# Full-row second products in the attention scores of a hybrid decoder trunk

## The chip, the cores and the metric

The kernel runs on one core of one Trainium2 chip. The metric is the device time of one execution in microseconds (us). A core has a matrix engine (PE, with its weight loads shown as PEld), a vector engine (DVE), a scalar engine (ACT), GpSimd (POOL) and a queue for transfers (SP). Each of them takes its instructions in the program's order, and they wait for each other through semaphores.

## The reference, cut to what matters

The trunk has two layers for 512 tokens of width 1024: a pooling layer with a convolutional gated feed-forward, then differential attention with a second feed-forward. The part at issue is the attention's scores. Each of 8 heads has two queries and two keys (c = 0, 1) of 64 channels:

```python
def block(args):
    qi, i = args
    s = jnp.einsum('bqchd,bkchd->bchqk', qi, k).astype(jnp.float32) * sm_scale
    qpos = i * Q_BLOCK + jnp.arange(Q_BLOCK)
    mask = kpos[None, :] <= qpos[:, None]
    s = jnp.where(mask, s, jnp.finfo(jnp.float32).min)
    p = jax.nn.softmax(s, axis=-1)
    attn = p[:, 0] - lam_full * p[:, 1]
    return jnp.einsum('bhqk,bkhe->bqhe', attn.astype(v.dtype), v)
```

A block is 128 queries, so there are 4 blocks a head and 32 units (h, qi) in all; block qi looks at the first (qi + 1) x 128 keys.

## The kernel before

All large products split each operand into a high and a low part, whose sum is the operand, and take three products of the parts (`mm3`, lines 158 to 160: high x high, high x low, low x high). PE's order is written out by hand; the order of DVE, ACT, POOL and SP in the attention is made by a scheduler when the program is built.

`heads(p)` makes the queries and keys of two heads, p in 0 to 3. Both projections come out with the channels of head 2p on partitions 0 to 63 (`lower`) and those of head 2p + 1 on 64 to 127 (`upper`). For the query, one tile `qs` of 128 rows holds the high part on the head's own half and the low part on the other half. For the key there are two kinds of tile: `kh`, one for each head, that holds the high part on both halves, and `kl`, one for both heads, that holds the low part of each head on its own half. So the scores of one unit and one c are two products into one bank, in `scores`:

```python
nc.tensor.matmul(ps[:, :m], qs[h, c][:, q], k1[:, :m], start=True, stop=False)
nc.tensor.matmul(ps[:, :m], qs[h, c][hi, q], k2[hi, :m], start=False, stop=True)
```

The first (line 526) contracts 128 rows: (query high + query low) x key high. The second (line 527) contracts the head's own 64 rows: query high x key low. `m` is 256, 256, 384 and 512 columns for qi = 0 to 3. A unit thus has four products on PE, one after the other: high and low for c = 0, high and low for c = 1.

The softmax of a unit runs on DVE (line 531, scale, mask and maximum, one for each c), ACT (line 533, the exponential) and DVE again (lines 538 to 540, the difference of the two softmaxes into `e`). The loop over the units takes at step i the scores of unit i, then some steps of a `filler` (projections of later heads `pj_q` and `pj_k`, values `pv`, the output product `pw`), then the transposes `pa` of unit i - 2 (line 549), the products `po` of unit i - 3 with the values (line 556) and, for the last block of a head, two steps later the transposes `pt` of that head's normed output `on` (line 574).

Before each projection POOL multiplies the 128x1024 chunk of weights by the norm's gain (line 479, `raw_q` and `raw_k`). It also takes the reciprocal root in each head's norm (lines 180 and 181, `r_o`), for which DVE's `on` (line 568) waits. Nothing else runs on POOL while the scores are taken.

Tiles of 128x512 such as `qs`, `kh` and `kl` come from one pool with the tag T and 44 slots. At the end of the first feed-forward its activations fill all 44. A slot is free for a new tile when the last reader of the tile before it has run.

Of the kernel before, what the change touches and what calls it, by code (L numbers as in the profile page):

```python
# [8 lines left out]
F32 = mybir.dt.float32  # L9
# [32 lines left out]
def constants():  # L42
    """What depends on shapes alone: the identity; the causal mask, whose last 128 columns are a
    diagonal block (rows are queries, columns keys); and for each pooling window the matrices, rows
    tokens in and columns tokens out, that take the mean over the window less the token: within the
    first tile of tokens, within a later one, and from the tile before it."""
    import numpy as np

    a = np.arange(P)
    back = a[None, :] - a[:, None]  # L50
    mask = np.zeros((P, S), np.float32)
    mask[:, S - P:] = np.where(back > 0, np.float32(NEG), np.float32(0))
    first, later, before = [], [], []
    for w in WINDOWS:
        near = (back >= 0) & (back < w)
        count = np.minimum(a + 1, w)[None, :]
        first.append(np.where(near, 1 / count, 0) - np.eye(P))
        later.append(np.where(near, 1 / w, 0) - np.eye(P))
        before.append(np.where(back[:, :16] + P < w, 1 / w, 0))
    return np.concatenate([np.eye(P), mask, *first, *later, *before], axis=1).astype(np.float32)  # L60
# [3 lines left out]
def trunk(ctx, tc, x, norm_g, pool_w, pool_scale, kv_norm, w_kv, wq, lam, subln_g, wo,  # L64
          w_up, conv_w, conv_b, w_down, final_norm, consts, out):
    nc = tc.nc
# [11 lines left out]
    def big(name, dt=F32R):  # L78
        return tp.tile([P, S], dt, tag="T", bufs=44, name=name)
# [13 lines left out]
    def spread(v, n):  # L93
        """[128, a] as [128, a, n]"""
        return v.unsqueeze(2).to_broadcast([P, v.shape[1], n])

# [1 line left out]
    xt = [const.tile([P, D], F32, name=f"x{t}") for t in range(NT)]  # L98
# [14 lines left out]
    def across(src, name):  # L113
        """A vector over the channels, on every partition, in halves."""
        halves = [big(f"{name}{i}", F32) for i in range(2)]
        for i in range(2):
            nc.sync.dma_start(out=halves[i], in_=src[i * S:(i + 1) * S].unsqueeze(0).to_broadcast([P, S]))
        return halves

    # TensorE's clock rises with its use  # L120
    ones = const.tile([P, P], F32, name="ones")
# [16 lines left out]
    def split(src, hi, lo):  # L138
        """hi + lo is src exactly, each in the 12 bits that one pass of TensorE carries."""
        nc.scalar.copy(hi, src)  # L140
        nc.vector.tensor_tensor(lo, src, hi, ALU.subtract)  # L141

    def split_scaled(src, by, hi, lo):
        """The same of src times a scalar for each partition."""
        nc.scalar.activation(hi, src, AF.Copy, scale=by)
        nc.vector.scalar_tensor_tensor(lo, src, by, hi, ALU.mult, ALU.subtract)

    def chunk(src, a, b, name):
        """[128, a, b] of weights, and where their parts go."""
        raw = wp.tile([P, a * b], F32, tag="raw", bufs=3, name=f"raw_{name}")  # L150
        hi = wp.tile([P, a * b], F32R, tag="hi", bufs=5, name=f"hi_{name}")
        lo = wp.tile([P, a * b], F32R, tag="lo", bufs=5, name=f"lo_{name}")
        nc.sync.dma_start(out=v3(raw, a), in_=src)
        return raw, hi, lo
# [10 lines left out]
    def columns(loaded):  # L165
        """Per-channel vectors, loaded as rows, with a channel a partition."""
        r, n, name = loaded
        ps = bank(f"pv_{name}")
        nc.tensor.transpose(ps[:, :n], r[:n, :], ident[:n, :n])
        c = const.tile([P, n], F32, name=f"c_{name}")  # L170
        nc.vector.tensor_copy(c, ps[:, :n])
        return c

    def rstd_of(ssq, n, name, eps=None):
        """From the mean of the squares."""
        r = small([P, n], f"r_{name}")
        if eps is None:
            nc.gpsimd.tensor_scalar(r, ssq, EPS, None, ALU.add)
        else:
            nc.gpsimd.tensor_tensor(r, ssq, eps, ALU.add)  # L180
        nc.gpsimd.tensor_tensor(r, r, halfneg[:, :n], ALU.pow)
        return r

    def rms(t, name):
        """One over the root mean square of x[t], and room for x[t]."""
        sq = wide(f"sq_{name}{t}")
        ssq = small([P, 1], f"ssq_{name}{t}")
        nc.scalar.activation(sq, xt[t], AF.Square, scale=D ** -0.5, accum_out=ssq)
        return rstd_of(ssq, 1, f"{name}{t}"), [sq[:, :S], sq[:, S:]]

    def normed(t, r, h, g=None):
        """x[t] over its root mean square, tokens on partitions, in halves of the channels."""
        for i in range(2):
            c = slice(i * S, (i + 1) * S)
            if g is None:
                nc.vector.tensor_scalar(h[i], xt[t][:, c], r, None, ALU.mult)
            else:
                nc.vector.scalar_tensor_tensor(h[i], xt[t][:, c], r, g[i], ALU.mult, ALU.mult)

    class Normed:  # L200
        """Normed x, channels on partitions, split; a tile of tokens at a time, in the steps rms,
        scale, turn and split."""

# [48 lines left out]

# [1 line left out]
    pscale = across(pool_scale[0], "pscale")  # L254
# [92 lines left out]

    # The steps, by tile of tokens, group of channels or chunk of weights, in the order in which
    # each engine takes its part of them.
    steps = dict(a=pool_rms, h=pool_scaled, g=gains, m=pool_weights, x=pool_weights_split, i=pool_in,  # L350
# [6 lines left out]

# [1 line left out]
    def ffn(l, hT, cw, ws, pss, after):  # L359
        """`pss` hold the first products, with `ws`, for half of the tokens. after(t, half) is called  # L360
        when that half of x[t] is done."""
        act = []
# [69 lines left out]

# [1 line left out]
    gkv, gsub = shared  # L434
# [12 lines left out]
    lamf = const.tile([P, 1], F32, name="lamf")  # L447
    # minus lambda
    nc.vector.tensor_tensor(lamf, lexp[:, 1:2], lexp[:, 0:1], ALU.subtract)
# [41 lines left out]
    def heads(p):  # L491
        """Queries and keys of two heads. A query's parts lie on the two halves of the partitions,
        and the keys' high parts on both, so that one product takes both parts of the query."""
        for c in range(2):
# [8 lines left out]
            ps = yield from project(w_kv[:, col:col + P], gkv, f"k{p}{c}")  # L503
            k2 = big(f"kl{p}{c}")
            for i, hi, lo in ((0, lower, upper), (1, upper, lower)):
                k1 = big(f"kh{p}{c}{i}")
                nc.scalar.copy(k1[hi], ps[hi])
                nc.scalar.copy(k1[lo], ps[hi])
                nc.vector.tensor_tensor(k2[hi], ps[hi], k1[hi], ALU.subtract)
                ks[2 * p + i, c] = (k1, k2, hi)  # L510
            yield
# [3 lines left out]
    def scores(h, qi):  # L515
# [7 lines left out]
        for c in range(2):  # L523
            ps = bank(f"sc{h}{qi}{c}")
            k1, k2, hi = ks[h, c]
            nc.tensor.matmul(ps[:, :m], qs[h, c][:, q], k1[:, :m], start=True, stop=False)  # L526
            nc.tensor.matmul(ps[:, :m], qs[h, c][hi, q], k2[hi, :m], start=False, stop=True)  # L527
            # minus the scaled scores, and minus their maximum
            e = e01[:, c * S:(c + 1) * S]
# [5 lines left out]
            e2.append(e[:, :n])  # L535
        # In units of the first softmax's sum, of which sub_norm takes account.
        r = small([P, 1], f"rs{h}{qi}")
# [85 lines left out]

    # The steps of the blocks of queries are taken apart, and other products put between them, so
    # that TensorE need not wait for the softmax.
    filler = chain(lambda: heads(1), lambda: heads(2), lambda: value_steps(1), lambda: heads(3),
# [6 lines left out]
    def behind(i):  # L633
        """The later steps of earlier blocks, at step i."""
        u = i - VALUES
# [14 lines left out]
    def wo_last():  # L650
        """What does not need the last head for the first two tiles of tokens."""
        wo_weights(6)
        wo_weights(7)
        for t in range(2):
            for dh in range(2):
                begun[t, dh] = bank(f"pw6{t}{dh}")
                wo_part(begun[t, dh], t, dh, 6, True, False)
                yield 0.25
# [99 lines left out]
```

## Time and profile before

| | us |
|---|---|
| median of 3 runs | 1044.49 |
| lowest and highest run | 1044.32 and 1048.61 |
| span of the profiled execution | 1043.1 |
| PE busy in the span | 1031.1 (99%) |
| DVE busy | 571.1 (55%) |
| ACT busy | 428.1 (41%) |
| POOL busy | 78.3 (8%) |

The profiled execution is one execution on the chip. Its span reaches from its first to its last instruction, so the span is compared with spans and the median with medians. A PE row of the timeline begins where the product begins, or where its weight load begins if PE had to wait for that load; its end is modelled, and rows overlap. What a product takes of PE's time is read from the distance between the starts of neighbouring rows, not from the row's own length.

### The profile page before, as it was taken

How to read it: one execution, taken by the hardware profiler on the slowest of the kernel's cores; microseconds unless marked ns; L12 is line 12 of the kernel's file. 1: busy time of each engine (PE TensorE's matmuls, PEld its weight loads, DVE VectorE, ACT ScalarE, POOL GpSimd, SP SyncE). 2: the span in 40 equal slices, each digit the busy share in tenths (PEclk: the TensorE clock that was granted, in tenths of full speed). 3: DMA queues.
4: the chain of work that ended last, by engine and by line, in shares of the span. 5: the costliest groups of instructions: out<-in, count | busy, mean ns of one | idle time of the engine just before them, and what ended most of it. 6: DMA issues, size and time to landing. Idle time of an engine off the chain costs nothing.

```text
span 1043.1 us, 12315 instructions
## 1 busy us (share of the span) xinstructions
PE 1031.1 (99%) x4871; PEld 843.4 (81%) x4871; DVE 571.1 (55%) x873; ACT 428.1 (41%) x671; POOL 78.3 (8%) x97
## 2 busy tenths in 40 slices
PE   8999999999999999999999999999999999999997
PEld 8988888888888887877777777898888888888885
DVE  5776566565621325366756676866656656532313
ACT  5454434443421124356545653444443444322211
POOL 4500000000000003330210000100000000000001
PEclk8999999999999999999999999999999999999999
DMA  8333333333323322241203102243333233323312
GB/s 250 106 109 93 101 101 88 95 101 101 93 94 101 93 99 81 65 138 61 62 21 101 61 21 61 67 116 90 93 101 100 88 95 101 101 82 100 101 41 80
DMA packets 128707, 95.33 MB, mean 91 GB/s; under 512 B 3329, under 2 KB 111498, under 8 KB 128650
## 3 DMA queue, kind: packets, MB, share of 16 engines
q1 hardware_dynamic: 128650, 94.55, 29.8%
q8 instruction: 38, 0.62, 0.2%
q14 instruction: 19, 0.16, 0.1%
HBM read 92.44 MB, written 2.10 MB: 91 GB/s over the span
## 4 chain that ended last, share of the span: by engine, by line
PE 97%; DVE 1%; DMA 1%; POOL 0%; ACT 0%; SPq 0%; issue 0%; DVEq 0%; POOLq 0%; ACTq 0%
PE pu L158 16%; PE pu L159 15%; PE pu L160 15%; PE pd L158 8%; PE pd L159 8%; PE pd L160 8%; PE sc L527 2%; PE po L556 2%; PE pj_k L158 2%; PE sc L526 2%; PE pw L158 2%; PE pj_q L158 2%; PE pw L160 1%; PE pj_k L160 1%; PE pj_q L159 1%; PE pj_q L160 1%
## 5 line engine op out<-in xcount | busy, mean ns | idle before, releaser
L141 DVE TENSOR_TENSOR lo_u<-raw_u,hi_u 128x1024 fp32r<-128x1024 f32 x84 | 103.0, 1229 | 130.5 <-ACT hi_u L140 130.5
L158 PE MATMUL pu<-n1h,hi_u 128*128 128x512 f32 (+1 forms) x384 | 144.1, 375 | 0.0
L159 PE MATMUL pu<-n3l,hi_u 128*128 128x512 f32 (+1 forms) x384 | 144.0, 375 | 0.0
L158 PE MATMUL pu<-n3h,hi_u 128*128 128x512 f32 (+1 forms) x384 | 143.6, 374 | 0.0
L160 PE MATMUL pu<-n1h,lo_u 128*128 128x512 f32 (+1 forms) x384 | 143.3, 373 | 0.0
L160 PE MATMUL pu<-n3h,lo_u 128*128 128x512 f32 (+1 forms) x384 | 142.1, 370 | 0.0
L159 PE MATMUL pu<-n1l,hi_u 128*128 128x512 f32 (+1 forms) x384 | 142.0, 370 | 0.0
L158 PE MATMUL pd<-hi_d,ah 128*128 128x512 f32 x352 | 138.8, 394 | 0.0
L159 PE MATMUL pd<-lo_d,ah 128*128 128x512 f32 x352 | 138.7, 394 | 0.0
L160 PE MATMUL pd<-hi_d,al 128*128 128x512 f32 x352 | 138.7, 394 | 0.0
L141 DVE TENSOR_TENSOR lo_d<-raw_d,hi_d 128x1024 fp32r<-128x1024 f32 x44 | 53.9, 1226 | 152.7 <-ACT hi_d L140 152.7
L140 ACT CAST hi_u<-raw_u 128x1024 fp32r<-128x1024 f32 x84 | 88.0, 1050 | 68.0 <-PE pu L159 62.9
L140 ACT CAST hi_d<-raw_d 128x1024 fp32r<-128x1024 f32 x44 | 46.1, 1048 | 148.0 <-PE pd L160 136.5
L158 PEld LDWEIGHTS pu<-n3h,hi_u 128*128 128x128 f32 x384 | 72.1, 188 | 14.1
L160 PEld LDWEIGHTS pu<-n1h,lo_u 128*128 128x128 f32 x384 | 72.0, 188 | 14.1
L160 PEld LDWEIGHTS pu<-n3h,lo_u 128*128 128x128 f32 x384 | 72.1, 188 | 13.4
L159 PEld LDWEIGHTS pu<-n1l,hi_u 128*128 128x128 f32 x384 | 72.1, 188 | 13.4
L158 PEld LDWEIGHTS pu<-n1h,hi_u 128*128 128x128 f32 x384 | 72.2, 188 | 12.0
L159 PEld LDWEIGHTS pu<-n3l,hi_u 128*128 128x128 f32 x384 | 72.2, 188 | 11.9
L160 PEld LDWEIGHTS pd<-hi_d,al 128*128 128x128 f32 x352 | 65.8, 187 | 16.3
L158 PEld LDWEIGHTS pd<-hi_d,ah 128*128 128x128 f32 x352 | 65.8, 187 | 16.3
L159 PEld LDWEIGHTS pd<-lo_d,ah 128*128 128x128 f32 x352 | 65.8, 187 | 16.2
(148 smaller groups left out, 1570.6 us busy)
## 6 DMA issues: line engine op xcount, KB each, us to landing
raw_u<-in_w_up_dram SPq DMA_DIRECT2D x88, 512.0 KB, 3.9
raw_d<-in_w_down_dram SPq DMA_DIRECT2D x44, 512.0 KB, 3.4
raw_v<-in_w_kv_dram SPq DMA_DIRECT2D x8, 512.0 KB, 3.5
raw_q<-in_wq_dram SPq DMA_DIRECT2D x8, 512.0 KB, 4.0
raw_k<-in_w_kv_dram SPq DMA_DIRECT2D x8, 512.0 KB
raw_o<-in_wo_dram SPq DMA_DIRECT2D x8, 512.0 KB, 4.1
x<-in_x_dram SPq DMA_DIRECT2D x4, 512.0 KB
out_dram<-y SPq DMA_DIRECT2D x8, 256.0 KB, 2.1
```

What stands on the lines that cost most here:

```text
L140: nc.scalar.copy(hi, src)
L141: nc.vector.tensor_tensor(lo, src, hi, ALU.subtract)
L158: nc.tensor.matmul(ps, lh, rh, start=first, stop=False)
L159: nc.tensor.matmul(ps, lh, rl, start=False, stop=False)
L160: nc.tensor.matmul(ps, ll, rh, start=False, stop=last)
L526: nc.tensor.matmul(ps[:, :m], qs[h, c][:, q], k1[:, :m], start=True, stop=False)
L527: nc.tensor.matmul(ps[:, :m], qs[h, c][hi, q], k2[hi, :m], start=False, stop=True)
L556: nc.tensor.matmul(po[h][:, qi * P:(qi + 1) * P], aT[:, kt * P:(kt + 1) * P], vt[kt][h // 4][:, (h % 4) * VD:(h % 4 + 1) * VD], start=kt = ...
```

## The change

The key's low part gets a tile for each head. The half that belongs to the head holds the low part, and the other half is set to zero by POOL (a new line 507, which makes 16 instructions of 64x512). The second product of the scores then takes all 128 rows: the other rows of the query meet zeros. The number of products, their columns and their order are as they were. The comments and docstrings are blanked out too, which adds one line ahead of `heads`' loop, so line 509 of before is line 510 of after, and lines 526 and 527 become one line 527.

```diff
             ps = yield from project(w_kv[:, col:col + P], gkv, f"k{p}{c}")
-            k2 = big(f"kl{p}{c}")
             for i, hi, lo in ((0, lower, upper), (1, upper, lower)):
-                k1 = big(f"kh{p}{c}{i}")
+                k1, k2 = big(f"kh{p}{c}{i}"), big(f"kl{p}{c}{i}")
+                nc.gpsimd.memset(k2[lo].bitcast(F32), 0.0)
                 nc.scalar.copy(k1[hi], ps[hi])
                 nc.scalar.copy(k1[lo], ps[hi])
                 nc.vector.tensor_tensor(k2[hi], ps[hi], k1[hi], ALU.subtract)
-                ks[2 * p + i, c] = (k1, k2, hi)
+                ks[2 * p + i, c] = (k1, k2)
...
-            k1, k2, hi = ks[h, c]
-            nc.tensor.matmul(ps[:, :m], qs[h, c][:, q], k1[:, :m], start=True, stop=False)
-            nc.tensor.matmul(ps[:, :m], qs[h, c][hi, q], k2[hi, :m], start=False, stop=True)
+            for last, k in enumerate(ks[h, c]):
+                nc.tensor.matmul(ps[:, :m], qs[h, c][:, q], k[:, :m], start=not last, stop=bool(last))
```

The order of the instructions on PE, DVE, ACT and SP stays as it was; 16 instructions join POOL's. On PE the first unit of scores stands as follows before (`sc` is the bank, `kh` and `kl` the key tiles, the size is that of the output):

```order
L160 MATMUL pj_q_3412<-n2h,lo_q_3407 128x512
L526 MATMUL sc_3427<-kh_3314,qs_3275 128x256
L527 MATMUL sc_3427<-kl_3313,qs_3275 128x256
L526 MATMUL sc_3433<-kh_3393,qs_3354 128x256
L527 MATMUL sc_3433<-kl_3392,qs_3354 128x256
```

The same place of the changed program:

```order
L160 MATMUL pj_q_3418<-n2h,lo_q_3413 128x512
L527 MATMUL sc_3433<-kh_3313,qs_3275 128x256
L527 MATMUL sc_3433<-kl_3314,qs_3275 128x256
L527 MATMUL sc_3439<-kh_3395,qs_3357 128x256
L527 MATMUL sc_3439<-kl_3396,qs_3357 128x256
```

The four products keep their places; the numbers in the names differ because more tiles are made. On POOL, in the stretch in which the first three pairs of heads are projected, before:

```order
L479 TENSOR_TENSOR raw_k_3596<-raw_k_3596,c_gkv 128x1024
L479 TENSOR_TENSOR raw_q_3686<-raw_q_3686,c_gn 128x1024
L479 TENSOR_TENSOR raw_k_3751<-raw_k_3751,c_gkv 128x1024
L479 TENSOR_TENSOR raw_q_3853<-raw_q_3853,c_gn 128x1024
L479 TENSOR_TENSOR raw_k_3925<-raw_k_3925,c_gkv 128x1024
```

And of the change:

```order
L479 TENSOR_TENSOR raw_k_3605<-raw_k_3605,c_gkv 128x1024
L507 MEMSET kl_3314 64x512
L479 TENSOR_TENSOR raw_q_3698<-raw_q_3698,c_gn 128x1024
L507 MEMSET kl_3320 64x512
L479 TENSOR_TENSOR raw_k_3763<-raw_k_3763,c_gkv 128x1024
L507 MEMSET kl_3396 64x512
L479 TENSOR_TENSOR raw_q_3868<-raw_q_3868,c_gn 128x1024
L507 MEMSET kl_3402 64x512
L479 TENSOR_TENSOR raw_k_3940<-raw_k_3940,c_gkv 128x1024
L507 MEMSET kl_3517 64x512
```

One zeroing instruction now stands between neighbouring chunks; of these, `kl_3314` and `kl_3396` are read by the second and the fourth product of the first unit above. Late in the attention, among the norms of heads 2, 3 and 4, POOL has before:

```order
L180 TENSOR_TENSOR r_o_4240<-os_4236,oe_4238 128x4
L181 TENSOR_TENSOR r_o_4240<-r_o_4240,halfneg 128x4
L180 TENSOR_TENSOR r_o_4446<-os_4442,oe_4444 128x4
L181 TENSOR_TENSOR r_o_4446<-r_o_4446,halfneg 128x4
L180 TENSOR_TENSOR r_o_4668<-os_4664,oe_4666 128x4
```

And of the change:

```order
L181 TENSOR_TENSOR r_o_4258<-r_o_4258,halfneg 128x4
L507 MEMSET kl_4499 64x512
L180 TENSOR_TENSOR r_o_4464<-os_4460,oe_4462 128x4
L181 TENSOR_TENSOR r_o_4464<-r_o_4464,halfneg 128x4
L507 MEMSET kl_4505 64x512
L507 MEMSET kl_4666 64x512
L507 MEMSET kl_4672 64x512
L180 TENSOR_TENSOR r_o_4692<-os_4688,oe_4690 128x4
```

The last four zeroings, for heads 6 and 7, stand ahead of the norms of heads 3 and 4. Each zeroing waits in the built program for the last reader of the tile that had its slot before: the first twelve for products `pd` of the first feed-forward, the last four for score products of heads 1 to 3 with qi = 3.

## The prediction

> **What bounds the kernel now.** The page comes first, for the engine that sets the end; then the busy time by stage, for the stage that the change touches; then the timeline of PE inside one unit of scores.
>
> ```profile
> span 1043.1 us, 12315 instructions
> ...
> PE 1031.1 (99%) x4871; PEld 843.4 (81%) x4871; DVE 571.1 (55%) x873; ACT 428.1 (41%) x671; POOL 78.3 (8%) x97
> ...
> PE 97%; DVE 1%; DMA 1%; POOL 0%; ACT 0%; SPq 0%; issue 0%; DVEq 0%; POOLq 0%; ACTq 0%
> ```
>
> The chain of work that ended last is 97% PE. So a microsecond taken off PE's order is a microsecond off the end, as long as nobody else becomes late. The view of stages (each row: stretch, its length, busy time of PE, PEld, DVE, ACT, POOL) shows how much room the others have:
>
> ```profile
> 458.47:485.27 26.80, 26.80 (x110) 19.65 (x109) 17.57 (x46) 15.35 (x36) 3.19 (x2) 1.00 0.30 98
> ...
> 601.57:618.01 16.44, 16.44 (x83) 12.17 (x82) 12.06 (x39) 8.79 (x23) 1.20 (x2) 1.00 0.00 1
> 618.01:633.06 15.05, 15.05 (x77) 11.04 (x76) 12.34 (x38) 8.12 (x22) 0.41 (x2) 1.00 0.24 71
> ```
>
> These are the first five units of scores and the units of heads 6 and 7, four each. PE has no gap in any of them and its granted clock is 1.00, so PE waits for nobody there. But a PE row that is called busy is not a PE at its peak. The timeline of PE and PEld around the first unit shows it:
>
> ```profile
> 458.24 0.39 PE L160 MATMUL pj_q<-n2h,lo_q 128*128 128x512 f32 x1
> 458.24 0.19 PEld L526 LDWEIGHTS sc<-kh,qs 128*128 128x128 f32 x1
> 458.47 0.27 PE L526 MATMUL sc<-kh,qs 128*128 128x256 f32 x1
> 458.67 0.18 PEld L527 LDWEIGHTS sc<-kl,qs 64*128 64x128 f32 x1 [0.24 <-issue]
> 458.67 0.38 PE L527 MATMUL sc<-kl,qs 64*128 64x256 f32 x1
> 458.98 0.19 PEld L526 LDWEIGHTS sc<-kh,qs 128*128 128x128 f32 x1
> 458.98 0.39 PE L526 MATMUL sc<-kh,qs 128*128 128x256 f32 x1
> 459.29 0.38 PE L527 MATMUL sc<-kl,qs 64*128 64x256 f32 x1
> 459.61 0.50 PE L158 MATMUL pj_q<-n2h,hi_q 128*128 128x512 f32 x1
> 459.94 0.39 PE L159 MATMUL pj_q<-n2l,hi_q 128*128 128x512 f32 x1
> ```
>
> Look at the loads. The load for the first `kh` product starts at 458.24, beside the projection before it, and is over when that product starts at 458.47: it is hidden. The load for the 64-row `kl` product starts only at 458.67, together with its product, and so does that of the next `kh` product at 458.98. The starts lie 0.20, 0.31, 0.31, 0.32 and 0.33 us apart. What such products take when every load is hidden is read where 128-row products follow each other:
>
> ```profile
> 672.08 0.28 PE L159 MATMUL pu<-n3l,hi_u 128*128 128x256 f32 x1
> ...
> 673.96 0.28 PE L160 MATMUL pu<-n3h,lo_u 128*128 128x256 f32 x1
> 478.26 0.39 PE L159 MATMUL pj_k<-n2l,hi_k 128*128 128x512 f32 x1
> ...
> 480.56 0.40 PE L160 MATMUL pj_k<-n2h,lo_k 128*128 128x512 f32 x1
> ```
>
> Sixteen steps of 256 columns take 673.96 - 672.08 = 1.88 us, 0.1175 each; ten of 512 columns take 2.30 us, 0.23 each. For 384 columns I take the middle, 0.174 (an estimate from these two). So the first `kh` product loses 0.08 us, each of the next three 0.19, and the projection behind the last loses 0.10, its load. The loss stands at each of the four places in a unit where the row count changes between 128 and 64, and at no step between equal counts in these rows.
>
> **The change part by part.** On PE the four changes of row count in each unit go. Nothing is added there: as many products, of as many columns. From the first row of a unit to the second product behind it, the four widths and both kinds of neighbours in front are:
>
> ```profile
> 469.23 0.33 PE L526 MATMUL sc<-kh,qs 128*128 128x384 f32 x1
> ...
> 470.93 0.39 PE L159 MATMUL pj_q<-n2l,hi_q 128*128 128x512 f32 x1
> ...
> 476.24 0.48 PE L526 MATMUL sc<-kh,qs 128*128 128x512 f32 x1
> ...
> 504.01 0.36 PE L526 MATMUL sc<-kh,qs 128*128 128x256 f32 x1
> ...
> 505.57 0.39 PE L159 MATMUL pj_q<-n2l,hi_q 128*128 128x512 f32 x1
> ...
> 640.98 0.48 PE L158 MATMUL pw<-hi_o,oh 128*128 128x512 f32 x1
> ...
> 641.76 0.39 PE L158 MATMUL pw<-hi_o,oh 128*128 128x512 f32 x1
> ```
>
> 256 columns behind a projection: 459.94 - 458.47 = 1.47 now, and 4 x 0.1175 + 0.23 = 0.70 then, so 0.77 goes. 256 columns behind the `po` products (504.01): 1.56 now. Here not all goes: the row at 640.98, the first product behind `po` in a place without scores, needs 0.78 for three products in place of 0.69, so 0.09 belongs to `po` and stays; 1.56 - 0.70 - 0.09 = 0.77. 384 columns: 470.93 - 469.23 = 1.70, less 4 x 0.174 + 0.23 = 0.93, is 0.77. 512 columns behind `pa` (476.24 to the row at 478.26 above): 2.02 - 5 x 0.23 - 0.09 = 0.78. There are as many units of each width as this row halved, since a unit has two such products:
>
> ```profile
> L527 PE MATMUL sc<-kl,qs x64: 377/408/501, 458.7 to 630.8; 64*128 64x256 f32 x32, 64*128 64x384 f32 x16, 64*128 64x512 f32 x16
> ```
>
> The sum is 16 x 0.77 + 8 x 0.77 + 8 x 0.78 = **24.7 us**.
>
> The Trainium skill speaks for and against this. "TensorEngine Tiling (Array Packing)", section Key Properties, says that a change of the tiling mode drains the engine; by it the loss at each change goes, as in the sum. "TensorE: Matmul & The Clock Gate", section The mechanism of its Part 3, says that a load overlaps products in flight only when its row group differs; by it the full-row product could hide nothing and the gain would be 0. The trace is against the second rule: the load at 458.24 lies beside a product on the same 128 rows and is hidden.
>
> POOL gets 16 zeroings of 64x512. The trace has none of that size; the nearest rows are these:
>
> ```profile
> L106 POOL MEMSET halfneg<- x1: 104/104/104, 0.7 to 0.7; 128x8 f32 x1
> ...
> L479 POOL TENSOR_TENSOR raw_q<-raw_q,c_gn x8: 1896/1898/2879, 395.8 to 520.1; 128x1024 f32<-128x1024 f32 x8
> L141 DVE TENSOR_TENSOR lo_q<-raw_q,hi_q x8: 1218/1224/2719, 410.8 to 555.8; 128x1024 fp32r<-128x1024 f32 x8
> ```
>
> At least 0.10 us, at most half of 1.90, which has twice the columns and two inputs: 0.95. I take 0.5, 8 us in all on an engine that is 8% busy. The rows also show that POOL and DVE can hold each other up: the longest `raw_q` took 0.98 more and the longest `lo_q` 1.5 more than the median. Counted at the full 0.95 for each zeroing that is 15 us of DVE over the 175 us from 458 to 633, and in the first stage above DVE idles a third of the time; it costs nothing, and if that cover were gone, up to those 15 us. What matters is whether a zeroing is late for PE or keeps POOL's next instruction waiting:
>
> ```profile
> 406.44 0.39 PE L160 MATMUL pd<-hi_d,al 128*128 128x512 f32 x1
> ...
> 452.76 1.90 POOL L479 TENSOR_TENSOR raw_k<-raw_k,c_gkv 128x1024 f32<-128x1024 f32 x1 [2.24 <-DMA raw_k<-in_w_kv_dram]
> ...
> 549.88 0.49 PE L527 MATMUL sc<-kl,qs 64*128 64x512 f32 x1
> ...
> 574.62 1.01 POOL L181 TENSOR_TENSOR r_o<-r_o,halfneg 128x4 f32<-128x4 f32 x1
> ```
>
> The tightest early one, `kl_3396`, stands behind this `raw_k`, so it ends by 454.66 + 0.95 = 455.6, with 3.0 us left to the first score at 458.47. POOL idled 2.24 us ahead of this chunk, waiting for its transfer, and a zeroing fits into such gaps. The slots of the first twelve come from `pd` products, the last of which started at 406.44. The last four come from scores of heads 1 to 3, whose last product started at 549.88; POOL reaches the last three of them at 575.6, 26 us later. So no zeroing waits. Eight more tiles in the pool thus cost 0; a slot that came 26 us later would begin to cost.
>
> When PE is faster, DVE is late next. A unit is 0.77 us shorter, so the stretch 618.01:633.06 shrinks from 15.05 to 11.97, while DVE is busy for 12.34 in it; 601.57:618.01 shrinks to 13.36 with 12.06 of DVE. DVE falls behind by at least 12.34 - 11.97 = 0.4 us in the last head and by at most 3.08, if none of its idle time shrinks. How much lag PE bears is read where it next needs DVE:
>
> ```profile
> 633.89 0.69 DVE L568 TENSOR_TENSOR on<-po,r_o 128x512 f32<-128x512 f32 x1 [0.79 <-POOL r_o L181]
> 636.00 0.75 DVE L540 SCALAR_TENSOR_TENSOR e<-e,rs 128x512 f32<-128x512 f32 x1
> 636.71 0.60 PE L574 MATMUL pt<-ident,on 128*128 128x128 f32 x4
> 639.95 0.60 PE L549 MATMUL pa<-ident,e 128*128 128x128 f32 x4
> ```
>
> The last `e` ends at 636.75 and is needed at 639.95, 3.2 us later; `on` of head 6 ends at 634.58 and is needed at 636.71, 2.13 later. One unit lies between, so 2.4 and 1.36 remain. PE waits between 0 and 3.08 - 1.36 = 1.7 us. I take 0, nearer to the smaller lag, since most of DVE's idle time there ends with PE and shrinks with it.
>
> **The sum.** The profiled span goes from 1043.1 to 1018.4. The median of the runs, 1044.49, lies 1.4 above the span; the difference is taken as it is: 1044.49 - 24.7 = **1019.8 us**.
>
> **The rivals.** *The loss is not one of the row count* and stays: 1044.5. For it: the `kl` products differ from the others in more than rows (their weights are the tile that was just loaded, their bank the one just written). Against it: `mm3` also loads the same weights twice in a row into one bank (lines 158 and 159), and its rows lie 0.23 apart. *The load stays exposed because the product before it lies on the same rows*: then each of the four loads that starts late now starts late afterwards too, and the time is 1044.5. Against it stands the load at 458.24, hidden beside a product on the same rows, and each step of 0.1175. It is what the second rule of the Trainium skill above would give. *Half of it goes*: only the drain or only the exposed load hangs on the row count; with about half of 24.7 left, 1032. Against it: both appear and vanish together in all of the rows above. *DVE becomes the bound* in heads 6 and 7, where it has 24.4 us of work for 25.3 us of PE: if its waits for ACT and POOL stay, those eight units give nothing, 8 x 0.77 = 6.2 back: 1026.0. For it: 96% is close; against it: the lag is borne for up to 1.36 us and there is room behind. *Slower:* a zeroing heads POOL's queue and waits for its slot, `r_o` of head 4 behind it waits, DVE stops at `on`, PE at `pt`. It decides if the slot comes over 26 us later than in the trace; each us beyond the margin is one on PE. To end slower by over 0.5% (about what a measurement can tell from no change, 5.2 us) it has to cost 30 us: 1050. The rows speak against it.
>
> **How the numbers follow.** Forecast, 1019.8: 0.81. DVE as the bound, 1026: 0.07. Half, 1032: 0.03. No effect, 1044.5: 0.07, of which 0.02 for loads that stay exposed on equal rows. Slower, 1050: 0.02. Faster is 0.81 + 0.07 + 0.03 = 0.91, same 0.07, slower 0.02. The range reaches down to 1017.2, if the 0.09 behind `po` and `pa` went too in 29 units (2.6 us), and up to 1026.0, which takes in the DVE case and a run that lies 4.1 above its median as the highest before did.
>
> **What would show it.** Right: `sc` rows with 128 rows in both kinds, 0.12, 0.17 and 0.23 us apart; the load of each `kl` product beside the product before it; the product behind the last `sc` 0.23 from its next; no idle time of PEld ended by "issue" at the scores. The zeroings each below 1 us, and PE without waits for POOL. DVE's idle time in heads 6 and 7 nearly gone. Wrong: the same 0.31 steps with 128 rows; or gaps of PE that end with DVE `on` or `e`; or POOL rows idle for a PE product ahead of a zeroing.

## The result and the profile after

| | before | after |
|---|---|---|
| median of the runs, us | 1044.41 (4 runs) | 1019.41 (4 runs) |
| lowest and highest run, us | 1044.32 and 1048.61 | 1018.22 and 1019.86 |
| span of the profiled execution, us | 1043.1 | 1017.7 |
| ratio of the times, 95% interval | | 0.9755, 0.9734 to 0.9776 |

The change makes the kernel 2.45% faster (2.2 to 2.7%); the prediction said 1019.8 us. The page of the changed kernel, the span first, then the busy time of each engine, then the chain that ended last:

```profile
span 1017.7 us, 12343 instructions
...
PE 1003.3 (99%) x4871; PEld 835.6 (82%) x4871; DVE 569.5 (56%) x873; ACT 427.1 (42%) x671; POOL 86.1 (8%) x113
...
PE 97%; DVE 1%; DMA 1%; issue 0%; SPq 0%; ACT 0%; DVEq 0%; POOLq 0%; POOL 0%; ACTq 0%
```

PE has the same 4871 products and is busy for 27.8 us less (1031.1 - 1003.3). POOL has 16 instructions and 7.8 us more. The chain is 97% PE, as before. The timeline of PE around a later unit of the changed kernel (a row: start and length in us, engine, line, operation, tiles, size):

```profile
477.60 0.39 PE L556 MATMUL po<-v,aT 128*128 128x128 f32 x2
477.74 0.36 PE L527 MATMUL sc<-kh,qs 128*128 128x256 f32 x1
477.94 0.29 PE L527 MATMUL sc<-kl,qs 128*128 128x256 f32 x1
478.06 0.28 PE L527 MATMUL sc<-kh,qs 128*128 128x256 f32 x1
478.18 0.28 PE L527 MATMUL sc<-kl,qs 128*128 128x256 f32 x1
478.30 0.39 PE L158 MATMUL pj_k<-n2h,hi_k 128*128 128x512 f32 x1
478.53 0.39 PE L159 MATMUL pj_k<-n2l,hi_k 128*128 128x512 f32 x1
```

The four products start 0.20, 0.12, 0.12 and 0.12 us ahead of the next row, and the projection behind them 0.23. What remains is 0.08 behind `po`, which the prediction had counted as staying. The first unit shows the load of a `kl` product, which now starts beside the `kh` product and 0.11 us ahead of its own:

```profile
456.46 0.27 PE L527 MATMUL sc<-kh,qs 128*128 128x256 f32 x1
456.46 0.19 PEld L527 LDWEIGHTS sc<-kl,qs 128*128 128x128 f32 x1
456.57 0.28 PE L527 MATMUL sc<-kl,qs 128*128 128x256 f32 x1
```

The stages, in the same columns as those of before (stretch, length, PE, PEld, DVE, ACT, POOL), between the same instructions:

```profile
456.46:481.06 24.60, 23.09 (x111) 19.11 (x109) 19.56 (x47) 15.04 (x36) 5.03 (x8) 1.00 0.33 107
582.41:595.75 13.34, 13.34 (x84) 11.63 (x82) 11.73 (x38) 8.91 (x25) 1.20 (x2) 1.00 0.00 1
595.75:607.68 11.93, 11.93 (x77) 10.49 (x76) 11.93 (x36) 8.09 (x22) 0.00 (x0) 1.00 0.31 90
```

Heads 6 and 7 went from 16.44 and 15.05 us to 13.34 and 11.93, and DVE is now busy for 11.93 of the last 11.93: it has no room left there, but PE has no gap. The first stretch is different: 26.80 became 24.60, though five units at 0.77 should give 3.85, and PE idles for 1.51 of it. The place is the first unit. The timeline of DVE, POOL and PE there, changed kernel:

```profile
454.63 1.90 POOL L479 TENSOR_TENSOR raw_q<-raw_q,c_gn 128x1024 f32<-128x1024 f32 x1 [1.90 <-DMA raw_q<-in_wq_dram]
454.77 2.84 DVE L141 TENSOR_TENSOR lo_q<-raw_q,hi_q 128x1024 fp32r<-128x1024 f32 x1 [2.31 <-ACT hi_q L140]
456.69 0.28 PE L527 MATMUL sc<-kh,qs 128*128 128x256 f32 x1
457.64 0.68 DVE L510 TENSOR_TENSOR kl<-pj_k,kh 64x512 fp32r<-64x512 f32 x1
458.47 0.35 PE L527 MATMUL sc<-kl,qs 128*128 128x256 f32 x1 [1.50 <-DVE kl L510]
458.67 0.40 PE L158 MATMUL pj_q<-n2h,hi_q 128*128 128x512 f32 x1
```

The last product of the unit waits 1.50 us for the low part `kl` of c = 1, which DVE starts only at 457.64, behind a `lo_q` of 2.84 us. The same place before:

```profile
456.78 1.23 DVE L141 TENSOR_TENSOR lo_q<-raw_q,hi_q 128x1024 fp32r<-128x1024 f32 x1 [1.86 <-ACT hi_q L140]
457.10 2.66 POOL L479 TENSOR_TENSOR raw_q<-raw_q,c_gn 128x1024 f32<-128x1024 f32 x1 [2.44 <-DMA raw_q<-in_wq_dram]
458.04 0.68 DVE L509 TENSOR_TENSOR kl<-pj_k,kh 64x512 fp32r<-64x512 f32 x1
```

There `lo_q` started first and took 1.23, and POOL's `raw_q` took 2.66; after, `raw_q` started first with 1.90, and `lo_q` took 2.84.

To see where the time came from, the starts of all PE rows of the two executions are set against each other, product by product (the order is the same in both). A unit is counted from the start of its first product to the start of the second product behind it. Gains in us: ahead of the first unit 2.0; in the first unit -0.97; in each of the 31 others 0.77 to 0.79, on the mean 0.78, together 24.2; between the units and behind them 0.1. The sum is 25.4, the difference of the spans. The 2.0 ahead of the first unit can't come from the products that were changed. 1.58 of it arises at one place, behind an `sq_n` of DVE. Timeline of before, then of after:

```profile
412.77 2.53 DVE L196 TENSOR_SCALAR sq_n<-x,r_n 128x512 f32<-128x512 f32 x2 [0.77 <-POOL r_n L181]
413.12 1.90 POOL L479 TENSOR_TENSOR raw_k<-raw_k,c_gkv 128x1024 f32<-128x1024 f32 x1 [0.38 <-DMA raw_k<-in_w_kv_dram]
415.95 0.50 PE L160 MATMUL pv<-hi_v,n2l 128*128 128x512 f32 x1 [1.31 <-DVE n2l L141]
```

```profile
412.31 0.88 DVE L196 TENSOR_SCALAR sq_n<-x,r_n 128x512 f32<-128x512 f32 x2 [0.76 <-POOL r_n L181]
412.88 2.06 POOL L479 TENSOR_TENSOR raw_k<-raw_k,c_gkv 128x1024 f32<-128x1024 f32 x1 [0.61 <-DVE sq_n L196]
```

Before, POOL's `raw_k` began at 413.12, while the first of the two `sq_n` of the row at 412.77 ran, and the pair took 2.53 in place of 0.88; PE then waited 1.31 us for `n2l`. After, `raw_k` stood behind DVE, and the place costs PE nothing. Whether this is part of the change is for the experiments.

### The profile page after: what moved, and what is told of

It is laid out like the page before. It is cut to its first block, busy times and chain, and to the rows that moved or that the text cites. A ratio compares the mean times of both kernels' runs of the same rounds, so it can differ in the third digit from the quotient of the medians.

```text
span 1017.7 us, 12343 instructions
## 1 busy us (share of the span) xinstructions
PE 1003.3 (99%) x4871; PEld 835.6 (82%) x4871; DVE 569.5 (56%) x873; ACT 427.1 (42%) x671; POOL 86.1 (8%) x113
## 4 chain that ended last, share of the span: by engine, by line
PE 97%; DVE 1%; DMA 1%; issue 0%; SPq 0%; ACT 0%; DVEq 0%; POOLq 0%; POOL 0%; ACTq 0%
PE pu L158 16%; PE pu L159 16%; PE pu L160 16%; PE pd L160 8%; PE pd L158 8%; PE pd L159 8%; PE sc L527 2%; PE po L556 2%; PE pw L160 1%; PE pv L158 1%; PE pv L160 1%; PE pv L159 1%; PE pj_k L159 1%; PE pj_k L158 1%; PE pw L159 1%; PE pw L158 1%
```

## The experiments

Seven runs were made, the sixth of them with the changed kernel itself. The first four came with one set of runs of the kernel before (median 1044.21, 13 runs), the next two with another (1045.09, 9 runs), the last with a third (1044.91, 7 runs). Gains "in a unit" are worked out as above, against the profiled execution of before.

**1. The tiles and zeroings alone.** Each head has its own zeroed tile, but the second product stays on 64 rows. Against the changed kernel:

```diff
-            for last, k in enumerate(ks[h, c]):
-                nc.tensor.matmul(ps[:, :m], qs[h, c][:, q], k[:, :m], start=not last, stop=bool(last))
+            k1, k2 = ks[h, c]
+            hi = upper if h % 2 else lower
+            nc.tensor.matmul(ps[:, :m], qs[h, c][:, q], k1[:, :m], start=True, stop=False)
+            nc.tensor.matmul(ps[:, :m], qs[h, c][hi, q], k2[hi, :m], start=False, stop=True)
```

> The changed kernel with its own tiles and its zeroings, but with the second product on the head's own 64 rows again; the result is the same. Theory (each change of row count between neighbouring products costs PE 0.19 us, four a unit): the whole 32 x 0.77 = 24.7 us comes back, about 1044.4 us, and the rows of the timeline lie 0.31 us apart at 256 columns as before. Rival (the gain came with the new tiles, where they lie or that each head has its own): it stays near 1019.4. A third reading, that zeroing and eight more tiles cost something that the gain hid, would show as a time above 1044.4; the theory allows at most 1 us for it.

Measured: 1045.44 us, ratio 1.0007 (0.9995 to 1.0018), span 1043.8. Units 1 to 31 differ by 0.00 from before; unit 0 is 0.84 longer, with a wait for `kl` as in the changed kernel. The timeline of PE around the second unit of this kernel:

```profile
465.95 0.28 PE L528 MATMUL sc<-kh,qs 128*128 128x256 f32 x1
466.16 0.38 PE L529 MATMUL sc<-kl,qs 64*128 64x256 f32 x1
466.47 0.38 PE L528 MATMUL sc<-kh,qs 128*128 128x256 f32 x1
466.79 0.38 PE L529 MATMUL sc<-kl,qs 64*128 64x256 f32 x1
467.10 0.50 PE L158 MATMUL pj_k<-n2h,hi_k 128*128 128x512 f32 x1
```

The 0.31 steps are back with the same tiles. So the whole gain is in the rows of the second product. The median is 1.2 us above that of before, a little over the 1 us that was allowed for, but its interval takes in no difference at all. Between the profiles it is 0.7 us, and the 0.84 of unit 0 accounts for it; experiment 2, which has neither these tiles nor zeroings, loses there too. So the tiles and zeroings cost nothing that the time shows.

**2. Half as many changes of row count.** The kernel before, with its 64-row products, in the order high, high, low, low, so that a unit has two changes in place of four. The scheduler also gave some instructions of DVE and ACT another order:

```diff
+        pair = [bank(f"sc{h}{qi}{c}") for c in range(2)]
+        for c in range(2):
+            nc.tensor.matmul(pair[c][:, :m], qs[h, c][:, q], ks[h, c][0][:, :m], start=True, stop=False)
...
-            nc.tensor.matmul(ps[:, :m], qs[h, c][:, q], k1[:, :m], start=True, stop=False)
-            nc.tensor.matmul(ps[:, :m], qs[h, c][hi, q], k2[hi, :m], start=False, stop=True)
+            nc.tensor.matmul(pair[c][:, :m], qs[h, c][hi, q], k2[hi, :m], start=False, stop=True)
```

> The kernel before, with the four products of a unit in another order: both high products first (128 rows), then both low products (64 rows). The result is the same; there are two changes of row count a unit in place of four. Theory (cost per change): half of the loss goes, 32 x 0.385 = 12.3 us, about 1032.1; the second low product's load is hidden behind the first. Rival A (each 64-row product exposes its own load, and so does the product behind it): three exposed loads of 0.19 stay, gain 32 x 0.19 = 6.1, about 1038.3. Rival B (the loss comes of loading the tile that was just loaded, or of the bank that was just written): both are now apart, so all goes, about 1019.8.

Measured: 1032.66 us, ratio 0.9875 (0.9854 to 0.9897), span 1030.7. Units 1 to 31 gain 0.37 to 0.40 each, half of 0.77; unit 0 loses 1.10. The same unit as above, with the loads of the low products:

```profile
464.91 0.40 PE L525 MATMUL sc<-kh,qs 128*128 128x256 f32 x2
465.23 0.29 PEld L528 LDWEIGHTS sc<-kl,qs 64*128 64x128 f32 x2
465.23 0.50 PE L528 MATMUL sc<-kl,qs 64*128 64x256 f32 x2
465.66 0.50 PE L158 MATMUL pj_k<-n2h,hi_k 128*128 128x512 f32 x1
466.00 0.39 PE L159 MATMUL pj_k<-n2l,hi_k 128*128 128x512 f32 x1
```

Two products of one kind stand in a row here (x2). Their single starts in the trace are 464.91 and 465.02 for the high ones and 465.23 and 465.46 for the low ones. The steps are thus 0.11, 0.21, 0.22 and 0.21 us, and 0.34 from the projection to the row at 466.00. Against 0.12 and 0.23 among full rows, each change costs about 0.20 us, half in the step ahead of it (0.09 and 0.09) and half in the step behind it, in which the load of the new kind is exposed (0.10 and 0.11). The 0.22 from the first low product to the second is such a step: the load that it shows is that of the first. The second low product's own load is hidden: the two loads end at 465.53, so the second one, of 0.19, starts at 465.34, beside the first low product and 0.11 ahead of its own, as among full rows. So a 64-row product behind a 64-row product on the same half adds nothing of its own. This also answers a rule of the Trainium skill ("TensorE: Matmul & The Clock Gate", section The mechanism of Part 3), by which a load overlaps a product in flight only if its row group differs: here the groups are equal and the load is hidden, and where a product of 64 rows meets one of 128 it is not.

**3. One of the two second products on full rows.** Only that of c = 0 takes 128 rows:

```diff
+                r = (upper if h % 2 else lower) if c and last else slice(0, P)
-                nc.tensor.matmul(ps[:, :m], qs[h, c][:, q], k[:, :m], start=not last, stop=bool(last))
+                nc.tensor.matmul(ps[:, :m], qs[h, c][r, q], k[r, :m], start=not last, stop=bool(last))
```

> The changed kernel with the full-row second product for c = 0 alone; for c = 1 it takes the 64 rows. The result is the same. Theory (cost per change of row count): two of the four changes stay, in front of and behind the last product of a unit, so half of the gain stays: about 1019.4 + 12.3 = 1031.7. Rival (the cost of a pair appears once a unit, whatever its number): 1019.4 or 1044.4.

Measured: 1033.26 us, ratio 0.9888 (0.9871 to 0.9905), span 1031.5. Units 1 to 31 gain 0.36 to 0.41, unit 0 loses 0.85. Two other changes of row count are gone than in the run above, at other places of the unit, and the gain is the same: the price goes by the number of changes. The 1.5 us above the expectation lie ahead of the scores: the expectation starts from the first run of the changed kernel, whose profile gained 2.0 there, and the profile of this kernel gains 0.3, with a `sq_n` pair of 2.60 us as before. Unit 0 loses about as much in both.

**4. Every zeroing twice.**

```diff
+                nc.gpsimd.memset(k2[lo].bitcast(F32), 0.0)
```

> The changed kernel with each zeroing on GpSimd done twice, 32 in place of 16, at 0.52 us each by the profile of the changed kernel; the result is the same. Theory (zeroing lies in GpSimd's idle time and nobody waits for it): the same time as the changed kernel, 1018 to 1021. Rival (zeroing holds DVE up, which shows in the 1.5 us that PE waited at the first unit of scores): each doubles, 2 to 8 us more, 1021 to 1027.

Measured: 1019.91 us, ratio 0.9761 (0.9743 to 0.9779), span 1019.4. Units 1 to 31 gain 0.75 to 0.80 as with one zeroing, and unit 0 loses 0.74. Sixteen more zeroings, 8.3 us of POOL, cost nothing that can be measured.

**5. The first unit one step later, and 6. the changed kernel again.** Experiment 5 moves the first unit of scores behind 12 more products of the projections, and the scheduler gave a few instructions of DVE and ACT around that unit another order; 6 is the changed kernel itself beside it on the same chip:

```diff
-START = 1
+START = 2
...
-    owed = 0.0
+    owed = -1.0
```

> The changed kernel, with the first unit of scores placed one step of filler (12 products of a projection, about 2.8 us) later; everything after it follows in the same order. Theory: in unit 0 TensorE waits 1.50 us for the low part `kl` because VectorE's `lo_q` (2.84 us) is held by GpSimd's `raw_q`; with 2.8 us more of projection ahead of the unit the low part is there in time, the wait is gone and nothing else is late: about 1.5 us less than the changed kernel on this chip, near 1017.9 us, and the low products of unit 0 wait for nothing over 0.2 us. Rival: VectorE's chain sets the time from here on, and the wait turns up again at a later place: the same time as the changed kernel within 0.5 us, with a new wait of TensorE of about 1.5 us in the first units.

> The changed kernel once more, unaltered, as the base of the run beside it: 1018 to 1021 us, a wait of TensorE of 0.8 to 1.5 us for `kl` in unit 0 under the theory that `lo_q` and `raw_q` hold each other up in every execution; under the rival that the stall of the first profile was a single mishap, no wait there and a unit 0 that gains 0.77 us like the others.

Measured: 5 took 1018.64 us (1018.39 to 1019.37), ratio 0.9741 (0.9726 to 0.9757), span 1016.9; 6 took 1020.31 (1018.23 to 1021.07), ratio 0.9752 (0.9734 to 0.9770), span 1019.3. The intervals overlap, so the times alone don't separate them; the traces do. In 6 the last product of unit 0 waits again:

```profile
456.16 1.90 POOL L479 TENSOR_TENSOR raw_q<-raw_q,c_gn 128x1024 f32<-128x1024 f32 x1 [1.71 <-DMA raw_q<-in_wq_dram]
456.34 2.80 DVE L141 TENSOR_TENSOR lo_q<-raw_q,hi_q 128x1024 fp32r<-128x1024 f32 x1 [2.20 <-ACT hi_q L140]
460.00 0.35 PE L527 MATMUL sc<-kl,qs 128*128 128x256 f32 x1 [1.46 <-DVE kl L510]
```

In 5 `lo_q` is held up as well, but the unit comes later and waits for nothing:

```profile
455.61 2.69 DVE L141 TENSOR_TENSOR lo_q<-raw_q,hi_q 128x1024 fp32r<-128x1024 f32 x1 [2.31 <-ACT hi_q L140]
458.33 0.68 DVE L510 TENSOR_TENSOR kl<-pj_k,kh 64x512 fp32r<-64x512 f32 x1
460.10 0.27 PE L527 MATMUL sc<-kh,qs 128*128 128x256 f32 x1
460.21 0.28 PE L527 MATMUL sc<-kl,qs 128*128 128x256 f32 x1
460.33 0.28 PE L527 MATMUL sc<-kh,qs 128*128 128x256 f32 x1
460.45 0.28 PE L527 MATMUL sc<-kl,qs 128*128 128x256 f32 x1
```

Unit 0 with its surroundings gains 0.74 in 5 and loses 0.93 in 6, 1.67 between them, and no new wait turns up in the later units, which gain 0.77 to 0.79 each. So the wait was real and not moved on. The rest of the 2.4 us between the spans lies ahead of the scores, where 5 lost 1.0 more in its first 30 us and saved 1.7 at the `sq_n` shown above: there the pair took 2.52 us in 6, as before, and 0.88 in 5. As 6 is the changed kernel itself, the 1.58 gained there in the first profile were not the change's doing.

**7. One multiplication left out.** What holds `lo_q`? This kernel leaves out POOL's `raw_q` by `c_gn` for the query weights of p = 2, c = 1:

```diff
-        nc.gpsimd.tensor_tensor(v3(raw, KD), v3(raw, KD), spread(g, P), ALU.mult)
+        name == "q21" or nc.gpsimd.tensor_tensor(v3(raw, KD), v3(raw, KD), spread(g, P), ALU.mult)
```

> The changed kernel without one instruction: GpSimd's multiply `raw_q` by `c_gn` for the query weights of p = 2, c = 1 (the one that began 0.14 us ahead of VectorE's `lo_q` in the profile of the changed kernel) is left out, so that these weights go in without their gain; nothing else moves. Theory: that `lo_q` takes 1.22 to 1.24 us in place of 2.84, the low part `kl` behind it is ready 1.6 us earlier, TensorE waits at most 0.2 us in unit 0, and unit 0 gains 0.6 us or more like the other 31; the time is about 1.5 us below the changed kernel, near 1018. Rival: `lo_q` is long for a reason of its own (the zeroings, or the projection's reads): it still takes 2.6 to 2.9 us, and the wait in unit 0 of 0.8 to 1.5 us stays.

Measured: 1018.02 us (1017.60 to 1020.03), ratio 0.9755 (0.9739 to 0.9772), span 1015.8. The time is near the 1018 expected, but its ratio is that of the changed kernel, so the times don't show the 1.5 us. The trace decides:

```profile
452.29 1.09 POOL L507 MEMSET kl<- 64x512 f32 x2
454.48 1.22 DVE L141 TENSOR_TENSOR lo_q<-raw_q,hi_q 128x1024 fp32r<-128x1024 f32 x1 [2.05 <-ACT hi_q L140]
455.74 0.68 DVE L510 TENSOR_TENSOR kl<-pj_k,kh 64x512 fp32r<-64x512 f32 x1
456.40 0.28 PE L527 MATMUL sc<-kh,qs 128*128 128x256 f32 x1
456.57 0.35 PE L527 MATMUL sc<-kl,qs 128*128 128x256 f32 x1
```

`lo_q` takes 1.22 us, `kl` is ready at 456.42, and unit 0 gains 0.65. The zeroings are still there, two of them ahead of this `lo_q`. So it was POOL's multiplication that held DVE, and not a zeroing. Experiment 2, which has no zeroings, has a `lo_q` of 2.85 us at the same place.

## Why the prediction was right, point by point

**What bounds it.** PE did: every gain on PE arrived at the end, and no other engine took its place.

**The loss at a change of row count.** Right, and shown from three sides: no change removed, 0.00 in a unit (experiment 1); two of four removed, 0.36 to 0.41 (2 and 3); all four removed, 0.75 to 0.80 (the changed kernel, its repeat, 4, 5 and 7). The sum counted 0.77 and 0.78; the mean was 0.78. The estimated 0.174 for 384 columns, taken as the middle of two rows, was right within that. The 0.09 behind `po` and `pa` stayed, as counted (0.08 measured). The rivals "not one of the row count" and "stays exposed on equal rows" fell with experiments 1 and 2, and "half of it goes" fell with the whole 0.78 of a unit. What was not tried is a change between two halves of 64 rows; so whether the count or the position of the rows sets the price is open.

**The zeroings.** Estimated at 0.5 us; the group of the changed kernel has all sixteen:

```profile
L507 POOL MEMSET kl<- x16: 518/520/524, 444.8 to 561.4; 64x512 f32 x16
```

That is 0.52, and neither one nor two of them cost time. The "slower" rival (a zeroing that waits for its slot) never appeared.

**DVE behind the faster PE.** The two stretches were to shrink to 13.36 and 11.97 and became 13.34 and 11.93. The lag was to leave margins of 2.4 us for `e` and 1.36 for `on`. The rows of the changed kernel:

```profile
609.24 0.69 DVE L568 TENSOR_TENSOR on<-po,r_o 128x512 f32<-128x512 f32 x1 [0.79 <-POOL r_o L181]
611.35 0.75 DVE L540 SCALAR_TENSOR_TENSOR e<-e,rs 128x512 f32<-128x512 f32 x1
611.35 0.60 PE L574 MATMUL pt<-ident,on 128*128 128x128 f32 x4
614.59 0.60 PE L549 MATMUL pa<-ident,e 128*128 128x128 f32 x4
```

`e` ends at 612.10, 2.5 ahead of `pa`; `on` ends at 609.93, 1.42 ahead of `pt`. The 0 taken out of 0 to 1.7 was right, and the rival of 1026 fell.

**Where a term was mis-sized.** The step "POOL and DVE can hold each other up ... it costs nothing" was wrong for one place. It asked how much DVE time the zeroings could take, and set that against DVE's idle time in the whole stage. What mattered was one instruction: a `lo_q` held for 1.6 us directly ahead of a `kl` for which PE had little to spare. The prediction looked at the time `kl` had to spare on POOL's side, 3.0 us in its words (458.47 - 455.6 is 2.9). On DVE's side it had less: before, it ended at 458.04 + 0.68 = 458.72, and the product that reads it began at 459.29, 0.57 later; with the shorter steps of the change that product comes 0.47 earlier in its unit (0.35 behind the unit's start in place of 0.82), and 0.10 is left. A hold-up of 1.6 us goes past that almost whole. Unit 0 therefore lost 0.97 in place of gaining 0.77: 1.74 us. The zeroings had no part in it (experiment 7; experiment 2, which has none, lost 1.10 in unit 0 too). What has a part is who comes first: `raw_q` starts when its transfer lands and `lo_q` when ACT is done, 0.32 apart with `lo_q` ahead in the profile of before, 0.14 apart with `raw_q` ahead after. Why the order turned over was not settled; `raw_q` came first in each of the seven other profiled executions in which both were there. The kernel before has a single profile, so whether its other executions met the same hold-up is not known.

**The sum.** 24.7 for the spans and 25.4 measured agree better than the terms do: 25.0 from all 32 units at 0.78, less 1.74 in unit 0, plus 2.0 ahead of the scores that the change doesn't touch, plus 0.1. That the loss and the gain that were not forecast nearly cancel is luck. The repeat, without those 2.0 (it had 0.4 there), has a span 23.8 shorter than before. The medians of both, 1019.41 and 1020.31, lie within the range of 1017.2 to 1026.0.

## What to carry to other kernels

If products of fewer rows stand between full ones, the start-to-start distances show the price: here 0.19 us at a change, more than the 0.12 that a whole product of 256 columns takes. Padding with zeros to full rows removes it. Putting products of one row count behind each other removed half of it here and needs no more tiles. Before counting an interference of two engines as hidden by idle time, look for the one instruction on the slower side whose result the critical engine needs next.

## What was not expected of the hardware

DVE and POOL did not share their time when `lo_q` and `raw_q` met; the one that started second stood until the first was over. In the changed kernel `raw_q` ends at 456.53, and from there to the end of `lo_q` at 457.61 are 1.08 us, nearly all of its 1.22. In the profile of before it is the other way: `lo_q` ends at 458.01, and `raw_q` at 459.76, 1.75 later, of its own 1.90. The Trainium skill states it: "SBUF — State Buffer", section "SBUF: two separate sides", says that the pair of ports that the two share is a lock and that whichever starts first has it for the whole instruction; the runs agree. A zeroing, which reads nothing, did not show this: in the changed kernel the one from 456.47 to 456.99 lies almost whole inside those 1.08 us, and neither of the two held the other up.

Such a meeting is decided by 0.1 to 0.4 us, and so differs between executions of one kernel: the `sq_n` at 412 us was held in six of the nine profiled executions (before, the repeat and experiments 1 to 4), and PE waited 1.26 to 1.47 us behind it each time. The four runs of the changed kernel differ by as much, 1.64 us, so a single profile of this kernel can't show a gain below 2 us by its span alone.
